# A two-layer hybrid block on one core: other start addresses for SBUF tiles, weight rows and inner tiles

## The chip, the core and the metric

The kernel runs on one core of a Trainium2 chip. Its five engines run side by side: TensorE (PE in the profile; its weight loads are listed as PEld) multiplies, VectorE (DVE) and ScalarE (ACT) work element by element, GpSimd (POOL) does some side work, and SyncE (SP) issues the loads and stores. The metric is the device time of one execution in microseconds (us).

A tile in SBUF is a run of bytes at the same offset in each of 128 partitions. This change is about these offsets. "A start of 32" below means an offset that is 32 bytes past a multiple of 128.

## What is computed

Two layers of a block on 512 tokens of 1024 features. Each layer adds two normed sublayers to x: a mixer (dilated attention beside a two-way mLSTM) and a gated feed-forward with a short convolution.

```python
def reference(x, ...):
    for l in range(DEPTH):
        mixed = hybrid_mixer(rms_norm(x, mix_pre_g[l]), w_in[l], ...)
        x = x + rms_norm(mixed, mix_post_g[l])
        ff = conv_ffn(rms_norm(x, ffn_pre_g[l]), w_up[l], ...)
        x = x + rms_norm(ff, ffn_post_g[l])
    return x

def hybrid_mixer(hn, w_in, ...):
    aq, ak, av, mq, mk, mv, mo, gates = jnp.split(hn @ w_in, split_at, axis=-1)
    ...
    return jnp.concatenate([attn, mlstm], axis=-1) @ w_out

def conv_ffn(hn, w_up, conv_w, conv_b, w_down):
    u = depthwise_conv_centred(hn @ w_up, conv_w, conv_b)
    gate, val = jnp.split(u, 2, axis=-1)
    return (jax.nn.gelu(gate, approximate=True) * val) @ w_down
```

The mixer's projections have 3600 columns, the feed-forward is 2816 wide, and everything is float32.

## The kernel before

Activations lie with the feature on partitions and the 512 tokens along the row, eight tiles of 128 features each. To keep float32 accuracy with the faster float32r products, each operand is split into a high and a low part, and `mac` (L193 to L202) makes three matmuls for each product: high weights with high activations, low weights with high activations, high weights with low activations. Of a matmul's two operands the *weights* are loaded into the array ahead of it (128 columns), and the *moving* operand streams through (up to 512 columns).

**Weights.** `load_raw` (L129) brings a piece of 128 by 1024 numbers (512 KB) into one of three buffers `wraw`, on SP's queue, in the order of use. `split_w` (L138) casts it to `whi` on ScalarE (L153) and subtracts on VectorE (`lo_part`, L91) to get `wlo`; both come from rings of three buffers of 4096 bytes a partition, eight rows of 128 numbers. Row k of a piece is the weight operand of the k-th of eight products that add up into one output tile.

```python
hi = whi_p.tile([P, 8, P], F32R, tag="whi", name="whi")
lo = wlo_p.tile([P, 8, P], F32R, tag="wlo", name="wlo")
```

**Activations.** The normed operand of a sublayer's first products is in eight pairs `ah`, `al` (2048 bytes each, `act_parts`); the mixer's output projection reads pairs `cp`. In the feed-forward, `unit` (L1038) makes 22 pairs `hh`, `hl` out of the gate and the value, and these are the moving operand of the down projection. A few pieces of weights that are split ahead of time lie in other tiles: `wnx`, `wsp`, `wlh`/`wll`, `pth`/`ptl`.

**Stages of a layer.** The mixer's 28 projection tiles, with attention and mLSTM steps as side work between the products; the output projection (8 tiles); the up projection (44 tiles of 8 times 3 matmuls of 512 columns); the down projection (8 tiles of 22 times 3). Near a norm, tiles are made by halves of the tokens, so with 256 columns. The value projection (`proj_v`) turns roles round: `ah` and `al` are the weights, 128 tokens at a time, and two rows of `whi` or `wlo` together are the moving operand of 256 columns, one run of 1024 bytes. Its outputs are scaled on VectorE in `v_out` (L657, L658).

**Order.** The program is written out step by step; side work is put in behind so many products (`settle`, `Stream.pump`), and a scheduler then orders each engine's instructions by its estimates. In the up and down projections TensorE runs the products one behind the other.

**Places.** Tiles come from pools that place them one behind the other. The granule is 32 bytes, so tiles of small or odd size shift all that follow them. [...]

Of the kernel before, what the change touches and what calls it, by code (L numbers as in the profile page):

```python
# [25 lines left out]
RAW = 3  # L26
RING = 3
# [5 lines left out]
# per head: the order of its projections (mLSTM q and k, both values, attention q and k), and its attention's rate  # L33
# [3 lines left out]
# columns of the per-feature parameter array  # L37
# [8 lines left out]
# columns of the constant array  # L46
# [10 lines left out]

@with_exitstack
def tile_hybrid_block(ctx: ExitStack, tc: tile.TileContext, xt, w_in, w_g, w_out, w_up, w_down, par, cst, out):
    nc = tc.nc  # L60
    pool = lambda name, bufs=1, **kw: ctx.enter_context(tc.tile_pool(name=name, bufs=bufs, **kw))
# [76 lines left out]
    def split_w(alloc=None):  # L138
        """the next piece as exact high and low parts; alloc gives their place, n of the eight rows at a time."""
        if not raw_q:  # L140
            return None
        raw, nk = raw_q.popleft()
        parts = {}
        n = 8
        k = 0
        while k < nk:
            if alloc is None:
                hi = whi_p.tile([P, 8, P], F32R, tag="whi", name="whi")
                lo = wlo_p.tile([P, 8, P], F32R, tag="wlo", name="wlo")
            else:  # L150
                hi, lo, n = alloc()
            m = min(n, nk - k)
            nc.scalar.copy(out=hi[:, 0:m, :], in_=raw[:, k:k + m, :])  # L153
            lo_part(lo[:, 0:m, :], raw[:, k:k + m, :], hi[:, 0:m, :])
            for j in range(m):
                parts[k + j] = (hi[:, j, :], lo[:, j, :])
            parts["all"] = (hi, lo)
            k += m
        load_raw()
        return parts  # L160
# [18 lines left out]
    # work to be put into the program once the tensor engine has so many more rows of products before it  # L179
# [12 lines left out]
    def mac(ps, w, kk, rhs, first, last, cols=None):  # L192
        """ps += w[:, kk, :]^T rhs with both operands as exact high and low parts."""  # L193
        settle()
        clock[0] += 3 * (T if cols is None else cols.stop - cols.start)
        hi, lo = w[kk]
        rh, rl = rhs
        if cols is not None:
            rh, rl = rh[:, cols], rl[:, cols]
        nc.tensor.matmul(out=ps, lhsT=hi, rhs=rh, start=first, stop=False)  # L200
        nc.tensor.matmul(out=ps, lhsT=lo, rhs=rh, start=False, stop=False)  # L201
        clock[1] = nc.tensor.matmul(out=ps, lhsT=hi, rhs=rl, start=False, stop=last).ins  # L202

# [1 line left out]
    class Stream:  # L205
        """generators one after another, a step at a time behind the products that come before it."""
# [29 lines left out]
    def rsqrt(ms, n):  # L236
        """1/sqrt(ms) on [P, n], by a first guess from the exponent and Newton steps."""
        y = sm.tile([P, n], F32, tag=f"rs_y{n}", name="rs_y")
        a = sm.tile([P, n], F32, tag=f"rs_a{n}", name="rs_a")
        yi = y[:, :].bitcast(I32)  # L240
        nc.vector.tensor_scalar(yi, ms.bitcast(I32), -0.5, float(0x5F3759DF), op0=ALU.mult, op1=ALU.add)
        for _ in range(3):
            nc.vector.tensor_tensor(out=a, in0=y, in1=y, op=ALU.mult)
            nc.vector.scalar_tensor_tensor(out=a, in0=a, scalar=-0.5, in1=ms, op0=ALU.mult, op1=ALU.mult)
            nc.vector.scalar_tensor_tensor(out=y, in0=a, scalar=1.5, in1=y, op0=ALU.add, op1=ALU.mult)
        return y

    def rsqrt_cols(ms):
        """for the two columns of ms [P, 2]: RS / sqrt(ms), by a first guess from the exponent and Newton steps."""
# [9 lines left out]
        # a third-order step, a = y^2 ms within 7% of 1: (a^2 + C1 a + C0) y = s / sqrt(ms)  # L259
# [4 lines left out]
        # Newton's: (y^2 ms - 3 s^2) y = -2 s^3 / sqrt(ms)  # L264
# [7 lines left out]
    class Stats:  # L272
        """Sums of squares over the features: the first tiles add up beside the tensor engine, which sums over the
        partitions of that sum and of each of the last `own` tiles."""
# [7 lines left out]
        def add(self, src, n, hf):  # L282
            """the n-th of the KT tiles, for the tokens of one half or (None) both."""
# [17 lines left out]
        def flush(self, h):  # L301
            """what has come for a half until now, the sum of the first tiles ahead."""
            if self.sp[h] is None:
                self.sp[h] = t_ps()
                nc.vector.memset(self.sp[h][:, 0:2], EPS)
                self.sums(h, 1, self.acc[:, halves[h]])
            for g, n, sq in self.late:
                if g == h:
                    self.sums(h, n - KT + self.own + 2, sq)
            self.late = [e for e in self.late if e[0] != h]  # L310
# [6 lines left out]
        def rstd(self, hf):  # L317
            """[P, 2] for a half, a token per partition."""
# [6 lines left out]
    def row_of(r):  # L325
        """[P, 2] with a token per partition -> [P, 256] PSUM with the token along the row, in every partition."""
# [11 lines left out]
    def pre_operand(g, k, ops, st, hf):  # L338
        """x * g as parts, and the square of x into the statistics."""
        parts_of(g, k, ops, hf)  # L340
        st.add(x[k][:, slice(0, T) if hf is None else halves[hf]], k, hf)
# [29 lines left out]
    class Post:  # L371
        """x += norm(m) * g for each half of the tokens, and the next block's operand from the new x."""
# [9 lines left out]
        def put(self, k, src, cols=slice(0, T)):  # L382
            """an output tile times the norm's gain."""
# [30 lines left out]
    def first_group(ws, pss, xp, scale, extra=None):  # L414
        """the tiles whose operand is still being made: by halves of the tokens, all tiles beside each other."""
# [10 lines left out]
    def last_tiles(ws, kts, act, post, n0, also=None):  # L426
        """the last output tiles by halves of the tokens, so that the norm of the first half overlaps the second."""
# [18 lines left out]
    def mixer_first(l, xp, sp, G, more, whole=False):  # L446
# [12 lines left out]
        if whole:  # L459
            # the input comes tile by tile  # L460
# [20 lines left out]
    def mixer(l, xp, first, mp, post):  # L481
# [10 lines left out]
        # what picks a direction's and head's own rows for the decay products: the chunk's m and, below, the chunk  # L492
# [18 lines left out]
        def gates(ps):  # L511
# [14 lines left out]
            # index: direction, step, head; the backward direction's step j is chunk 3 - j  # L526
# [6 lines left out]
            # log sigmoid(f) = min(f, 0) - log1p(exp(-|f|)), the log1p as 2 atanh(e / (2 + e))  # L533
# [32 lines left out]
            # running maxima, forward for the first 16 rows and backward for the others  # L566
# [19 lines left out]
            # the state's maximum before each step, and with the step's own  # L586
# [16 lines left out]
            # keys are twice their value until here, and carry the scale  # L603
# [3 lines left out]
            # rows: -M and m_prev - M in the chunk's own columns, as parts  # L607
# [22 lines left out]
        def conv_out(ps, i, name):  # L630
            """five taps, then twice the silu."""
# [15 lines left out]
        def v_out(pss):  # L647
            """values of both kinds with the token on partitions: [P, chunk, kind, feature], two chunks in a bank."""
# [22 lines left out]
        def rot_out(ps, name):  # L671
# [12 lines left out]
            if name == "aq":  # L684
                # a head's high and low parts on top of each other
# [3 lines left out]
            else:  # L689
                # a head's high part twice, and the low parts of both heads  # L690
# [11 lines left out]
        def attn(hp):  # L702
# [3 lines left out]
            def scores(a, qt):  # L706
# [7 lines left out]
                # -(s + bias) / 8 and its minimum  # L714
# [46 lines left out]
        def mlstm(h):  # L761
# [3 lines left out]
            # keys with the token on partitions, times what enters the state  # L765
# [32 lines left out]
            # the part that each direction sees  # L798
# [8 lines left out]
            for d in range(2):  # L807
# [7 lines left out]
                # the masked half may overflow, and is nothing in sm_  # L815
# [43 lines left out]
        # projections; side work of the heads goes between them  # L859
# [3 lines left out]
        # streams of side work, each with its steps for each part of a projection tile  # L863
# [15 lines left out]
        def proj_v():  # L879
            """the tokens as the output's rows: both kinds of values beside each other."""  # L880
# [3 lines left out]
            for c in range(4):  # L884
# [3 lines left out]
                for k in range(KT):  # L888
                    hi, lo = (w[:, 2 * (k % 4):2 * (k % 4) + 2, :].rearrange("p i f -> p (i f)") for w in ws[k // 4])
# [40 lines left out]
        # output projection  # L930
# [91 lines left out]
    def ffn(l, xp, first, fp, post):  # L1022
# [16 lines left out]
        def unit(i, pg, pv):  # L1039
# [4 lines left out]
            hi = fp.tile([P, T], F32R, name=f"hh{i}")  # L1044
            lo = fp.tile([P, T], F32R, name=f"hl{i}")
# [53 lines left out]
        def next_place():  # L1099
            k = places.pop(0)  # L1100
            return (fp.tile([P, 4, P], F32R, tag=f"hh{k}", name="wnx"), fp.tile([P, 4, P], F32R, tag=f"hl{k}", name="wnx"), 4)
# [8 lines left out]
    # loads in the order in which the first products need them  # L1110
# [26 lines left out]
    for l in range(DEPTH):  # L1137
        with tc.tile_pool(name=f"mix{l}", bufs=1) as mp:
            post = Post(l, "mix_post", l, "ffn_pre", 2)
# [5 lines left out]
        with tc.tile_pool(name=f"ffn{l}", bufs=1) as fp:  # L1145
            post = Post(l, "ffn_post", l + 1, "mix_pre", 1)
# [6 lines left out]
def _constants():  # L1153
# [32 lines left out]
    # how many of the dilated patterns hold key - query, as a bias before the scale  # L1186
# [63 lines left out]
```

## Time and profile before

| | us |
|---|---|
| Two runs | 1391.45 and 1391.57, median 1391.51 |
| Profiled execution, span from the first to the last instruction | 1389.7 |
| Mixer and output projection, layer 0 (0 to 390): TensorE busy | 377.62 |
| Mixer and output projection, layer 1 (690 to 1080): TensorE busy | 381.87 |
| Median of the runs above the profiled span | 1.8 |

The profiled execution's time outside its span isn't listed apart; the two runs stand 1.75 and 1.87 us above the span. How to read the rows: a row of busy times gives each engine's busy time in a stretch and, in brackets, how many of its instructions touch it. A timeline row is a start, a duration, engine, line, operation, and output<-inputs. A matmul's duration includes its way through the array, during which the next ones run already; the tempo is the distance between starts. A row of groups gives a count, the busy time in us, the mean of one in ns, and the idle time ahead of it.

### The profile page before, as it was taken

What the parts mean: (1) busy time and instruction counts of PE and PEld (TensorE: products, weight loads), DVE (VectorE), ACT (ScalarE), POOL (GpSimd) and SP (SyncE); (2) the same over time, 40 slices, a digit from 0 to 9 for tenths busy, and PEclk for the clock granted to TensorE, in tenths of its full rate; (3) what the DMA queues carried; (4) which work ended last, traced back from release to release, by engine and by line L of the source; (5) the groups of instructions that cost most, each with busy time, mean ns of one, the idle gap of its engine ahead of it and who ended that gap; (6) DMA issues with size and microseconds to landing.
All of it is one profiled execution on the core that took longest, in us unless ns stands there. A gap on an engine that the chain in (4) does not pass through costs nothing. (4 is left out here: it accounts for less than half of the span.)

```text
span 1389.7 us, 18680 instructions
## 1 busy us (share of the span) xinstructions
PE 1359.0 (98%) x7152; PEld 1126.2 (81%) x7152; DVE 955.7 (69%) x1885; ACT 721.8 (52%) x1226; POOL 105.9 (8%) x110
## 2 busy tenths in 40 slices
PE   7999999999999999999999999999999999999997
PEld 6778878789888888888986888787898888888886
DVE  6989788747887777422498887778479777773233
ACT  5686686754544444323356766866546444442230
POOL 0000000024000000000120000000240000000102
PEclk9999999999999999999999999999999999999999
DMA  6212122140333333233311121122412333323221
GB/s 231 61 35 88 31 61 77 48 150 2 100 98 107 91 95 99 86 96 103 99 67 61 61 61 51 42 77 74 124 47 76 107 91 96 102 87 99 90 89 61
DMA packets 34089, 115.34 MB, mean 83 GB/s; under 512 B 3664, under 2 KB 6352, under 8 KB 34000
## 3 DMA queue, kind: packets, MB, share of 16 engines
q1 hardware_dynamic: 34000, 114.15, 27.0%
q8 instruction: 56, 0.92, 0.3%
q14 instruction: 33, 0.27, 0.1%
HBM read 112.04 MB, written 2.10 MB: 82 GB/s over the span
## 5 line engine op out<-in xcount | busy, mean ns | idle before, releaser
L91 DVE TENSOR_TENSOR wlo<-wraw,whi 128x1024 fp32r<-128x1024 f32 (+1 forms) x192 | 236.5, 1234 | 180.6 <-ACT whi L153 178.8
L200 PE MATMUL mm<-ah,whi 128*128 128x512 f32 (+1 forms) x880 | 342.0, 389 | 0.0
L201 PE MATMUL mm<-ah,wlo 128*128 128x512 f32 (+1 forms) x880 | 335.3, 381 | 0.0
L202 PE MATMUL mm<-al,whi 128*128 128x512 f32 (+1 forms) x880 | 334.1, 381 | 0.9 <-DVE al L348 0.8
L153 ACT CAST whi<-wraw 128x1024 fp32r<-128x1024 f32 (+1 forms) x192 | 197.6, 1034 | 168.6 <-PE mm L202 112.4
L200 PEld LDWEIGHTS mm<-ah,whi 128*128 128x128 f32 x880 | 166.5, 189 | 39.1 <-issue 12.0
L202 PEld LDWEIGHTS mm<-al,whi 128*128 128x128 f32 x880 | 166.2, 189 | 32.3 <-issue 1.9
L201 PEld LDWEIGHTS mm<-ah,wlo 128*128 128x128 f32 x880 | 166.6, 189 | 27.8 <-issue 1.9
L296 POOL TENSOR_TENSOR acc<-acc,sq 128x512 f32<-128x512 f32 x22 | 29.6, 1345 | 764.1 <-ACT sq L293 759.8
L200 PE MATMUL mm<-hh,whi 128*128 128x512 f32 x220 | 86.7, 394 | 0.0
L201 PE MATMUL mm<-hh,wlo 128*128 128x512 f32 x220 | 86.7, 394 | 0.0
L202 PE MATMUL mm<-hl,whi 128*128 128x512 f32 x220 | 86.7, 394 | 0.0
L1029 DVE TENSOR_TENSOR u<-mm,prow 128x512 f32<-128x512 f32 x64 | 43.8, 686 | 50.1 <-PE mm L202 39.6
L893 PE MATMUL mm<-whi,ah 128*128 128x256 f32 x256 | 74.4, 292 | 0.2 <-DVE cu L633 0.2
L1046 ACT CAST hh<-cv 128x512 fp32r<-128x512 f32 x44 | 27.3, 620 | 87.5 <-DVE cv L1043 87.5
L895 PE MATMUL mm<-whi,al 128*128 128x256 f32 x256 | 72.4, 283 | 0.0
L894 PE MATMUL mm<-wlo,ah 128*128 128x256 f32 x256 | 72.4, 283 | 0.0
L1041 ACT ACTIVATE cg<-cg 128x512 f32<-128x512 f32 x44 | 27.9, 633 | 74.5 <-DVE cg L1035 74.2
L201 PE MATMUL o<-ah,wlo 128*128 128x512 f32 (+1 forms) x160 | 60.6, 379 | 0.0
L200 PE MATMUL o<-ah,whi 128*128 128x512 f32 (+1 forms) x160 | 60.5, 378 | 0.0
L202 PE MATMUL o<-al,whi 128*128 128x512 f32 (+1 forms) x160 | 60.5, 378 | 0.0
L719 ACT ACTIVATE p<-p,mx 128x512 f32<-128x512 f32 x64 | 46.1, 720 | 21.6 <-DVE mx L716 21.6
(317 smaller groups left out, 2788.3 us busy)
## 6 DMA issues: line engine op xcount, KB each, us to landing
wraw<-in_w_up SPq DMA_DIRECT2D x88, 512.0 KB, 3.6
wraw<-in_w_in SPq DMA_DIRECT2D x56, 512.0 KB, 3.5
wraw<-in_w_down SPq DMA_DIRECT2D x32, 512.0 KB, 3.5
wraw<-in_w_out SPq DMA_DIRECT2D x16, 512.0 KB, 3.5
wraw<-in_w_down SPq DMA_DIRECT2D x16, 384.0 KB, 3.1
x<-in_xt SPq DMA_DIRECT2D x4, 512.0 KB, 7.3
out_dram<-x SPq DMA_DIRECT2D x8, 256.0 KB, 2.2
tb<-in_cst SPq DMA_DIRECT2D x2, 967.0 KB, 5.1
```

Source lines behind the costliest of these rows:

```text
L91: nc.vector.tensor_tensor(out=dst, in0=src, in1=f32v(hi), op=ALU.subtract)
L153: nc.scalar.copy(out=hi[:, 0:m, :], in_=raw[:, k:k + m, :])
L200: nc.tensor.matmul(out=ps, lhsT=hi, rhs=rh, start=first, stop=False)
L201: nc.tensor.matmul(out=ps, lhsT=lo, rhs=rh, start=False, stop=False)
L202: clock[1] = nc.tensor.matmul(out=ps, lhsT=hi, rhs=rl, start=False, stop=last).ins
L296: e.tensor_tensor(out=self.acc[:, cols], in0=self.acc[:, cols], in1=sq, op=ALU.add)
L719: nc.scalar.activation(out=p_, in_=p_, func=AF.Exp, scale=-1.0, bias=mx, accum_out=den)
L893: nc.tensor.matmul(out=o_, lhsT=xh, rhs=hi, start=(k == 0), stop=False)
L894: nc.tensor.matmul(out=o_, lhsT=xh, rhs=lo, start=False, stop=False)
L895: clock[1] = nc.tensor.matmul(out=o_, lhsT=xl, rhs=hi, start=False, stop=(k == KT - 1)).ins
L1029: nc.vector.tensor_tensor(out=u, in0=ps, in1=st["row"], op=ALU.mult)
L1041: nc.scalar.activation(out=g, in_=g, func=AF.Gelu_apprx_tanh)
```

## The change

Five things change; the comments that the diff also drops do nothing.

- Every pool is wrapped in `Aligned`, which rounds each tile's size up to a multiple of 128 bytes. As the first tile starts at 0 of 128, so do the rest.
- The rows of `whi` and `wlo` are 136 numbers apart and not 128 (544 bytes, buffers of 4352); 128 of them are used. The cast, the subtraction and the moving operand of the value projection so become patterns of eight (or two) runs.
- `hh` and `hl` come from the unwrapped pool with 520 numbers a row, so each starts 32 bytes further than the one before it, modulo 128. The same holds for the two pairs `wnx` that take their place at the end.
- The value projection takes its two rows as a two-dimensional pattern.
- The scratch area shrinks from 16384 to 1024 bytes. 218752 bytes a partition are taken then.

```diff
+LINE = 128
+STEP = 8
...
+class Aligned:
+    def __init__(self, pool):
+        self.pool = pool
+    def tile(self, shape, dtype, **kw):
+        n = 1
+        for s in shape[1:]:
+            n *= s
+        if n * 4 % LINE == 0:
+            return self.pool.tile(shape, dtype, **kw)
+        flat = self.pool.tile([shape[0], -(-n * 4 // LINE) * LINE // 4], dtype, **kw)[:, 0:n]
...
-    pool = lambda name, bufs=1, **kw: ctx.enter_context(tc.tile_pool(name=name, bufs=bufs, **kw))
+    pool = lambda name, bufs=1, **kw: Aligned(ctx.enter_context(tc.tile_pool(name=name, bufs=bufs, **kw)))
...
-                hi = whi_p.tile([P, 8, P], F32R, tag="whi", name="whi")
-                lo = wlo_p.tile([P, 8, P], F32R, tag="wlo", name="wlo")
+                hi = whi_p.tile([P, 8, P + STEP], F32R, tag="whi", name="whi")[:, :, 0:P]
+                lo = wlo_p.tile([P, 8, P + STEP], F32R, tag="wlo", name="wlo")[:, :, 0:P]
...
-                    hi, lo = (w[:, 2 * (k % 4):2 * (k % 4) + 2, :].rearrange("p i f -> p (i f)") for w in ws[k // 4])
+                    hi, lo = (w[:, 2 * (k % 4):2 * (k % 4) + 2, :] for w in ws[k // 4])
...
-            hi = fp.tile([P, T], F32R, name=f"hh{i}")
-            lo = fp.tile([P, T], F32R, name=f"hl{i}")
+            hi = fp.pool.tile([P, T + STEP], F32R, name=f"hh{i}")[:, 0:T]
+            lo = fp.pool.tile([P, T + STEP], F32R, name=f"hl{i}")[:, 0:T]
...
+            mp = Aligned(mp)
...
+            fp = Aligned(fp)
...
-    nc = bacc.Bacc("TRN2", target_bir_lowering=False, num_devices=1)
+    nc = bacc.Bacc("TRN2", target_bir_lowering=False, num_devices=1, dynamic_dma_scratch_size=1024)
```

Starts modulo 128 as the two programs place them:

| Tile | before | after |
|---|---|---|
| ah, al, wlh, wll, prow, wraw, x | 32 | 0 |
| whi, wlo: rows 0 to 7 | all 32 | 0, 32, 64, 96, 0, 32, 64, 96 |
| hh, of i even / odd | 96 | 0 / 64 |
| hl, of i even / odd | 96 | 32 / 96 |
| cp (in turn on mixer tiles) | 32, 64 or 96 | 0 |
| pth, ptl, and attention's aq, ak | 64 | 0 |
| vs | 0 | 0 |
| wnx where it stands in tb's place | 96 | 0 |

The order of TensorE's, ScalarE's, GpSimd's and SyncE's instructions stays as it is. On VectorE three instructions move back in each layer. The place is the value projection of one head, where VectorE scales the product `mm` by `rt` into the mLSTM's values `v` and the attention's values `vf`, between steps of the mLSTM's output (`r`, `hs`) and of a softmax (`p`, `mx`, `den`). Before:

```order
L840 TENSOR_TENSOR r_1712<-s,ex 128x2
L650 MEMSET v_1777 128x4
L657 TENSOR_TENSOR v_1777<-mm,rt 128x2x128
L841 SCALAR_TENSOR_TENSOR r_1712<-s,r_1712 128x2
L658 TENSOR_TENSOR vf<-mm,rt 128x256
L842 RECIPROCAL r_1712<-r_1712 128x2
L716 ISA p,mx<-s,tb 128x512
L716 ISA mx 128x1
L844 SCALAR_TENSOR_TENSOR hs<-s,r_1712,hs 128x128
L657 TENSOR_TENSOR v_1777<-mm,rt 128x2x128
L658 TENSOR_TENSOR vf<-mm,rt 128x256
L720 RECIPROCAL den<-den 128x1
```

After, with lines 21 higher:

```order
L861 TENSOR_TENSOR r_1712<-s,ex 128x2
L671 MEMSET v_1777 128x4
L862 SCALAR_TENSOR_TENSOR r_1712<-s,r_1712 128x2
L678 TENSOR_TENSOR v_1777<-mm,rt 128x2x128
L863 RECIPROCAL r_1712<-r_1712 128x2
L737 ISA p,mx<-s,tb 128x512
L737 ISA mx 128x1
L865 SCALAR_TENSOR_TENSOR hs<-s,r_1712,hs 128x128
L679 TENSOR_TENSOR vf<-mm,rt 128x256
L678 TENSOR_TENSOR v_1777<-mm,rt 128x2x128
L741 RECIPROCAL den<-den 128x1
L679 TENSOR_TENSOR vf<-mm,rt 128x256
```

The scaling of the first two chunks into `v` stands one step later, that into `vf` behind the softmax step and `hs`, and the last one behind `den`. Elsewhere on VectorE only forms change, as here at the end of a mixer, where weights are split (`wlo`) behind steps of the attention. Before:

```order
L823 SCALAR_TENSOR_TENSOR Q_2789<-Q_2789,mq 128x512
L720 RECIPROCAL den<-den 128x1
L666 TENSOR_TENSOR sg<-mm,prow 128x512
L91 TENSOR_TENSOR ptl<-t,pth 128x4x128
L91 TENSOR_TENSOR wlo<-wraw,whi 128x1024
```

After:

```order
L844 SCALAR_TENSOR_TENSOR Q_2789<-Q_2789,mq 128x512
L741 RECIPROCAL den<-den 128x1
L687 TENSOR_TENSOR sg<-mm,prow 128x512
L112 TENSOR_TENSOR ptl<-t,pth 128x4x128
L112 TENSOR_TENSOR wlo<-wraw,whi 128x8x128
```

Nothing moved; the subtraction is written in eight runs of 128 numbers and not in one of 1024.

More of the change, by code (lines that the diff above doesn't have):

```diff
@@ L55 @@
 NC1 = CC["rowmask"]
+class Aligned:
[8 more added lines that the diff above has]
+        flat = self.pool.tile([shape[0], -(-n * 4 // LINE) * LINE // 4], dtype, **kw)[:, 0:n]
+        if len(shape) == 2:
+            return flat
+        names = " ".join("abcd"[:len(shape) - 1])
+        return flat.rearrange(f"p ({names}) -> p {names}", **{c: s for c, s in zip("abcd", shape[1:-1])})
 @with_exitstack
@@ L1100, in next_place @@
             k = places.pop(0)
-            return (fp.tile([P, 4, P], F32R, tag=f"hh{k}", name="wnx"), fp.tile([P, 4, P], F32R, tag=f"hl{k}", name="wnx"), 4)
+            return (fp.pool.tile([P, T + STEP], F32R, tag=f"hh{k}", name="wnx")[:, 0:T].rearrange("p (k m) -> p k m", k=4), fp.pool.tile([P, T + STEP], F32R, tag=f"hl{k}", name="wnx")[:, 0:T].rearrange("p (k m) -> p k m", k=4), 4)
         def also():
```

## The prediction

> **What bounds the kernel.** I read the page's busy times first, then its chain of waits, then the stages in the windows view, and at last single starts in the timeline of TensorE.
>
> ```profile
> span 1389.7 us, 18680 instructions
> PE 1359.0 (98%) x7152; PEld 1126.2 (81%) x7152; DVE 955.7 (69%) x1885; ACT 721.8 (52%) x1226; POOL 105.9 (8%) x110
> q1 hardware_dynamic: 34000, 114.15, 27.0%
> PE 36%; DVE 2%; ACT 0%; issue 0%; DVEq 0%
> ```
>
> TensorE is busy in 1359.0 of 1389.7 us, and no other engine comes near. The chain's shares are small because it could follow only part of the span, but nearly all of what it followed is TensorE. So time can come only from the tempo of the matmuls, and a busy share of 98% doesn't tell that tempo: matmuls overlap, so the number to read is the distance from one start to the next. The stages give it.
>
> ```profile
> core 0: us, PE busy (x) PEld busy (x) DVE busy (x) ACT busy (x) POOL busy (x), PEclk, DMA share, GB/s
> 390.00:560.00 170.00, 170.00 (x752) 140.77 (x751) 125.75 (x160) 76.55 (x95) 0.00 (x0) 1.00 0.33 98
> 570.00:670.00 100.00, 100.00 (x430) 80.17 (x429) 28.09 (x26) 29.05 (x39) 6.48 (x5) 1.00 0.35 107
> ```
>
> The first stretch is the up projection, the second the down projection of layer 0; both are pure streams of matmuls of 512 columns at a granted clock of 1.00. Two of the counted matmuls reach into a stretch from before it, so 170.00 / 750 = 226.7 ns from start to start, and 100.00 / 428.5 = 233.3 ns. The instruction, its shapes and the weights' tiles are the same. VectorE is far busier in the faster stretch (125.75 of 170 us against 28.09 of 100), so the other engines don't make the difference. What differs is where the moving operand starts: ah and al at 32 past a multiple of 128 bytes, hh and hl at 96. The timeline shows the step at the change of stage.
>
> ```profile
> 564.62 0.39 PE L201 MATMUL mm<-ah,wlo 128*128 128x512 f32 x1
> ...
> 565.75 0.39 PE L200 MATMUL o<-hh,whi 128*128 128x512 f32 x1
> ...
> 566.45 0.39 PE L200 MATMUL o<-hh,whi 128*128 128x512 f32 x1
> ```
>
> Five starts in 1.13 us (226), then three in 0.70 (233), with nothing between. So the start address matters. Matmuls of 256 columns say the same of the weights' address:
>
> ```profile
> 328.87 0.28 PE L200 MATMUL mm<-ah,wnx 128*128 128x256 f32 x1
> ...
> 329.21 0.28 PE L200 MATMUL mm<-ah,whi 128*128 128x256 f32 x1
> ...
> 330.17 0.28 PE L202 MATMUL o<-al,whi 128*128 128x256 f32 x1
> 673.91 0.28 PE L200 MATMUL mm<-hh,wlh 128*128 128x256 f32 x1
> ...
> 675.27 0.28 PE L200 MATMUL mm<-hh,wlh 128*128 128x256 f32 x1
> ...
> 678.11 0.28 PE L200 MATMUL mm<-hh,wlh 128*128 128x256 f32 x1
> ...
> 679.52 0.28 PE L200 MATMUL mm<-hh,wlh 128*128 128x256 f32 x1
> ```
>
> From wnx (weights at 96) three starts take 0.34 us, 113.3 ns each; from whi (weights at 32) eight take 0.96, 120.0 each. With hh moving, twelve take 1.36 (113.3); after a break the same twelve take 1.41 (117.5), so what came before counts too. Take ah with whi: 226.7 for 512 columns and 120.0 for 256 leave 106.7 for 256 columns, hence 213.3 for 512 and a fixed 13.3 on each matmul. The pairs 233.3/226.7 and 120.0/113.3 differ by the same 6.67, so I count in steps of 6.67 ns: two with ah and whi, three with hh at 512 columns, one with hh and with wnx at 256. None of these has zero.
>
> **The change part by part.** By the kernel's allocation ah, al, cp and nearly all other tiles will start at 0 of 128; the eight rows of whi and wlo at 0, 32, 64, 96 and again; hh at 0 or 64, hl at 32 or 96. No row before shows a moving operand of 256 or more columns at 0, so the price has to be bounded. The counts:
>
> ```profile
> L200 PE MATMUL mm<-ah,whi 128*128 128x512 f32 x768 | 309.5, 403 | 0.0
> L200 PE MATMUL o<-ah,whi 128*128 128x512 f32 x144 | 56.0, 389 | 0.0
> L200 PE MATMUL mm<-hh,whi 128*128 128x512 f32 x220 | 86.7, 394 | 0.0
> L200 PE MATMUL o<-hh,whi 128*128 128x512 f32 x88 | 34.7, 394 | 0.0
> L200 PE MATMUL mm<-cp,whi 128*128 128x512 f32 x80 | 31.5, 398 | 0.0
> L200 PE MATMUL mm<-ah,whi 128*128 128x256 f32 x112 | 32.5, 292 | 0.0
> L893 PE MATMUL mm<-whi,ah 128*128 128x256 f32 x256 | 74.4, 292 | 0.2 <-DVE cu L633 0.2
> ```
>
> Each stands for three (L201 and L202, or L894 and L895, have the same counts): 2736 matmuls of 512 columns from ah, 924 from hh, 240 from cp, 336 of 256 columns from ah, and 768 of 256 columns in the value projection, where the weights move.
>
> - Aligned ah, al, cp. Lower end: all steps go, 13.3 ns x 2976 = 39.7 us. Upper end: a third step as with hh, 6.67 x 2976 = 19.8 us more. I take one step off, which is a guess between the two: a start at a boundary should save one partial read, while whatever the weight load adds stays. 2976 x 6.67 = 19.8 us.
> - hh and hl spread over four starts: lower end 20.0 x 924 = 18.5 us off, upper end one step more, 6.2 us. I take one step off (to the 226.7 that ah has at another start): 6.2 us.
> - 336 short matmuls from ah: 120.0 to 113.3 as wnx shows, 2.2 us; upper end nothing.
> - Value projection: the moving operand becomes two runs of 512 bytes, the second at another start. Lower end 6.67 off as above, upper end one step more, 5.1 us either way. I take zero, since it gains an aligned ah as weights and loses a single run.
> - Rows of the weights apart: the cast and the subtraction write eight runs instead of one. Nearest rows:
>
> ```profile
> L91 DVE TENSOR_TENSOR wlo<-wraw,whi 128x1024 fp32r<-128x1024 f32 x178 | 218.3, 1229 | 136.8 <-ACT whi L153 134.9
> L91 DVE TENSOR_TENSOR ptl<-t,pth 128x512 fp32r<-128x512 f32 x64 | 43.7, 683 | 9.4 <-ACT pth L730 9.1
> L91 DVE TENSOR_TENSOR hl<-cv,hh 128x512 fp32r<-128x512 f32 x44 | 30.4, 690 | 22.0 <-ACT hh L1046 22.0
> L658 DVE TENSOR_TENSOR vf<-mm,rt 128x256 f32<-128x256 f32 x16 | 6.7, 416 | 0.0
> ```
>
> ptl is written in four runs and takes 683, hl in one and takes 690; their tiles start at 64 and 96. So neither runs nor starts cost VectorE anything, and I cost this at nothing; the cover is VectorE's 26% of free time in the up projection, where a subtraction would have to grow from 1.2 us by some 1.4 us to be late (44 us free over 31 pieces of weights). The three VectorE instructions that move back in each layer's value projection are of this 416 ns size, stand between others of their kind, and cost nothing. TensorE's order is unchanged. [...]
>
> Sum: 19.8 + 6.2 + 2.2 = 28.2 us off. Against the profiled span, 1389.7 - 28.2 = 1361.5; the runs' median of 1391.5 stands 1.8 us above the span, so 1363.3, rounded to 1363. If TensorE gains 3% in the up projection, VectorE's share rises from 74 to some 76% there, so nothing else is late next.
>
> [...]
>
> **The rivals.** *All steps go* (1331): 39.7 + 18.5 + 2.2 = 60.4 us off. For it: nothing in the program forces the 13.3. Against: no settled stream in the trace is without a step.
>
> *No net gain* (1393, from 1385 to 1410). The steps depend on how the two reads fall against each other, and staggered rows never let the stream settle. The trace shows such a state after a break:
>
> ```profile
> 57.99 0.39 PE L201 MATMUL mm<-ah,wlo 128*128 128x512 f32 x1
> ...
> 59.60 0.39 PE L202 MATMUL mm<-al,whi 128*128 128x512 f32 x1
> ...
> 61.87 0.39 PE L200 MATMUL mm<-ah,whi 128*128 128x512 f32 x1
> ```
>
> Seven starts take 1.61 us (230), the next ten 2.27 (227). At 230 everywhere the two up projections lose 3.3 x 1500 = 5.0 us and hh gains 3.3 x 924 = 3.0: 1393.5. With a third step for all of ah, 1410. Against it: this was a passing state, with equal starts.
>
> *Addresses do nothing*, 1391.5. It comes to the same class as the last. Against it stands the step at 565.75. [...]
>
> *Slower* (1430): a weight row that starts off 128 costs the stream two steps more. It strikes six rows in eight in all projections, 0.75 x 3900 matmuls x 13.3 = 39 us. It decides from 27.8 / 2925 = 9.5 ns each. For it: three steps occur. Against: weights at 32 are the present state, and at 96 they were faster.
>
> **How the numbers follow.** One step off 0.40, all steps 0.20, no net gain or no effect 0.30, slower 0.10. The 2% line, about what a measurement of this kernel can tell from no change, is 27.8 us, and the likeliest sum lies on it; since its open ends (hh, value projection) reach further down, I give 0.25 of its 0.40 to the faster side. Faster 0.25 + 0.20 = 0.45, within 2% 0.15 + 0.30 = 0.45, slower 0.10. The range leaves out the slow case and the worst of no net gain: 1330 to 1400. The likeliest case's own range is 1350 to 1375.
>
> **What would show it.** In the profile after: 220 ns from start to start in the up projection (about 773 matmuls in 170 us), 226.7 in the down projection, wlo still at some 1230 ns. Starts that swing about 230 speak for no net gain, 213 to 216 for all steps gone, 233 or more in the up projection for the slow case. The prediction is wrong if the tempo doesn't change, or if VectorE's or ScalarE's splits grow by over a microsecond.

## The result, and the profile after

| | before | after |
|---|---|---|
| Runs, us | 1391.45, 1391.57 | 1398.81, 1400.06 |
| Median, us | 1391.51 | 1399.43 |
| Span of the profiled execution, us | 1389.7 | 1396.8 |
| Ratio of the times, 95% interval | | 1.0057, 1.0038 to 1.0075 |

The changed kernel takes 7.9 us more. That is small, but the interval of the ratio lies wholly above 1: the kernel got slower, where 1363 us had been forecast. The page of the changed kernel, its span, busy times, data queue and the chain's shares by engine:

```profile
span 1396.8 us, 18682 instructions
...
PE 1365.5 (98%) x7152; PEld 1125.7 (81%) x7152; DVE 956.6 (68%) x1885; ACT 718.1 (51%) x1226; POOL 105.9 (8%) x110
...
q1 hardware_dynamic: 34000, 114.15, 27.0%
...
PE 36%; DVE 2%; ACT 0%; issue 0%; DVEq 0%
```

TensorE is the bound as before. Its busy time rose by 6.5 us, the span by 7.1, and no other engine changed by more than 4 us. The windows view of the same two stretches, the up and the down projection of layer 0:

```profile
core 0: us, PE busy (x) PEld busy (x) DVE busy (x) ACT busy (x) POOL busy (x), PEclk, DMA share, GB/s
390.00:560.00 170.00, 170.00 (x736) 137.99 (x736) 122.83 (x155) 74.56 (x94) 0.00 (x0) 1.00 0.32 94
570.00:670.00 100.00, 100.00 (x433) 80.97 (x432) 30.81 (x30) 29.05 (x39) 6.47 (x5) 1.00 0.35 105
```

The clock is 1.00 in both, as it was. By the prediction's way of counting, the up projection went from 752 matmuls (226.7 ns from start to start) to 736 (170.00 / 734 = 231.6), and the down projection from 430 (233.3) to 433 (100.00 / 431.5 = 231.7). The two stages, 6.7 ns apart before, now have nearly one tempo, between their old ones. The timeline of TensorE shows it in the up projection:

```profile
401.38 0.40 PE L221 MATMUL mm<-ah,whi 128*128 128x512 f32 x1
401.62 0.40 PE L222 MATMUL mm<-ah,wlo 128*128 128x512 f32 x1
401.85 0.39 PE L223 MATMUL mm<-al,whi 128*128 128x512 f32 x1
402.08 0.39 PE L221 MATMUL mm<-ah,whi 128*128 128x512 f32 x1
...
402.77 0.39 PE L221 MATMUL mm<-ah,whi 128*128 128x512 f32 x1
...
403.46 0.39 PE L221 MATMUL mm<-ah,whi 128*128 128x512 f32 x1
```

Three rows of weights (nine starts) from 401.38 to 403.46 take 2.08 us, 231 ns a start, and nothing is idle between them. The groups by form, of those the prediction priced:

```profile
L112 DVE TENSOR_TENSOR wlo<-wraw,whi 128x1024 fp32r<-128x1024 f32 x178 | 218.4, 1230 | 139.3 <-ACT whi L174 139.2
...
L112 DVE TENSOR_TENSOR ptl<-t,pth 128x512 fp32r<-128x512 f32 x64 | 43.7, 683 | 9.3 <-ACT pth L751 9.1
...
L914 PE MATMUL mm<-whi,ah 128*128 128x256 f32 x256 | 74.0, 290 | 0.2 <-DVE cu L654 0.2
```

The subtraction that makes wlo takes 1230 ns where it took 1229, now that it writes eight runs. So the loss is in TensorE's tempo. Summed up from the starts in the two traces, each matmul's distance to the next, in us:

| Matmuls | before | after | difference |
|---|---|---|---|
| up projection, 512 columns (1920) | 435.9 | 444.5 | +8.6 |
| down projection, 512 columns (924) | 215.6 | 214.5 | -1.1 |
| mixers without the output projection, all 512 columns (1088), waits included | 305.3 | 304.3 | -1.0 |
| value projection (768) | 95.6 | 94.7 | -0.9 |
| down projection, 256 columns (264) | 31.8 | 32.3 | +0.5 |

Together they give +6.1 of the 7.1. The rest is spread thinly over the span and was not followed further. The mixers' products with ah and al also got slower: their distances under 260 ns rose from 230.2 to 231.9 in the mean. But fewer starts were held up for longer than that (190 before, 183 after, 74.1 and 70.3 us together), so nothing of it stays.

### The profile page after: what moved, and what is told of

It reads as the page before. It is cut to its first block, busy times and chain, and to the rows that moved or that the text cites. A ratio compares the mean times of both kernels' runs of the same rounds, so it can differ in the third digit from the quotient of the medians.

```text
span 1396.8 us, 18682 instructions
## 1 busy us (share of the span) xinstructions
PE 1365.5 (98%) x7152; PEld 1125.7 (81%) x7152; DVE 956.6 (68%) x1885; ACT 718.1 (51%) x1226; POOL 105.9 (8%) x110
```

## The experiments

Three questions stood: which part of the change loses, what a start really does, and whether one can do better. The expectations give the theories by letters. S: a stream is fastest only where moving operand and weights all have one start, the same from row to row. Z: a start at 0 is costly by itself. E: each matmul pays by its own pair of starts. N: what counts is the pair of the moving operand and the *next* weights, which are loaded while it streams (in the trace of the kernel before the weights of the matmul that starts at 400.06 us are loaded from 399.84, while the one that starts at 399.83 runs for 0.39 us). C: only starts modulo 256 bytes matter, and that the rows are written and read in separate runs costs nothing.

**The change in parts.** Alignment alone, without the rows' and hh's extra 32 bytes; the rows alone; hh and hl alone.

```diff
 # aligned alone, against the changed kernel
-STEP = 8
+STEP = 0
 # rows alone, against the kernel before
-                hi = whi_p.tile([P, 8, P], F32R, tag="whi", name="whi")
+                hi = whi_p.tile([P, 8, P + 8], F32R, tag="whi", name="whi")[:, :, 0:P]
...
-                    hi, lo = (w[:, 2 * (k % 4):2 * (k % 4) + 2, :].rearrange("p i f -> p (i f)") for w in ws[k // 4])
+                    hi, lo = (w[:, 2 * (k % 4):2 * (k % 4) + 2, :] for w in ws[k // 4])
 # hh and hl alone, against the kernel before (hl and wnx likewise)
-            hi = fp.tile([P, T], F32R, name=f"hh{i}")
+            hi = fp.tile([P, T + 8], F32R, name=f"hh{i}")[:, 0:T]
```

Aligned alone:

> Every tile at a start of 0, but no spread: weight rows 512 bytes apart again, hh and hl at 0. Theory S (successive weight rows with different starts keep the stream from settling): the up projection settles again at 226.7 ns from start to start, because moving and weights have equal starts as they had before; hh and weights have equal starts too, so the down projection settles at 226.7 instead of 233.3 and the time is about 1391.5 - 924 x 6.67 ns = 1385 us. Theory Z (the start at 0 is itself the costly one): the up projection stays at about 231 ns and the time near 1399 us.

Rows alone:

> The kernel before with only the weight rows 32 bytes further apart (and the smaller scratch, which makes the room); all other tiles at their old starts. Theory S: the up projection at about 231 ns, the down projection between 230 and 233, the time 1391.5 + 1500 x 4.5 ns, and a little more in the mixers, so 1397 to 1400 us. Theory Z: nothing was aligned, so 226.7 and 233.3 ns and 1391.5 us.

hh and hl alone:

> The kernel before with only hh and hl 32 bytes further apart each (and the smaller scratch). Theory S: the up projection settled at 226.7 ns as before; the down projection doesn't settle, and swings about 230 to 233 ns; the time within 2 us of 1391.5. Theory Z: the same up projection, the down projection a mean of four starts, somewhere from 226.7 to 233.3, so 1385 to 1391.5 us.

| | median, us | ratio to before, 95% interval |
|---|---|---|
| aligned alone | 1387.12 | 0.9968 (0.9956 to 0.9981) |
| rows alone | 1398.65 | 1.0052 (1.0037 to 1.0067) |
| hh and hl alone | 1390.65 | 0.9994 (0.9985 to 1.0004) |

The windows of aligned alone (the second one ends at 660, so that only 512 columns lie in it):

```profile
390.00:560.00 170.00, 170.00 (x752) 140.84 (x751) 125.43 (x160) 77.11 (x96) 0.00 (x0) 1.00 0.33 97
570.00:660.00 90.00, 90.00 (x399) 74.56 (x398) 26.27 (x25) 27.04 (x36) 6.46 (x5) 1.00 0.33 99
```

Rows alone:

```profile
390.00:560.00 170.00, 170.00 (x736) 137.89 (x735) 122.81 (x156) 74.58 (x94) 0.00 (x0) 1.00 0.32 95
570.00:670.00 100.00, 100.00 (x433) 81.04 (x432) 30.72 (x30) 29.48 (x40) 6.46 (x5) 1.00 0.35 103
```

hh and hl alone:

```profile
390.00:560.00 170.00, 170.00 (x752) 140.79 (x751) 125.44 (x160) 76.78 (x95) 0.00 (x0) 1.00 0.32 98
570.00:670.00 100.00, 100.00 (x432) 81.06 (x432) 28.35 (x27) 29.39 (x39) 6.49 (x5) 1.00 0.36 108
```

The rows alone give the changed kernel's counts (736 and 433) and its whole loss. Alignment alone is faster than before: the up projection stays at 752, since ah and the weights had one start before (32) and have one now (0), and the down projection comes to 90.00 / 397 = 226.7 ns, since hh and hl now start where the weights do. That is 6.67 ns x 924 = 6.2 us; the span fell by 6.0, the medians of the runs by 4.4, less than S had forecast (1385 us). The 264 products of hh with 256 columns, whose starts are now equal too, got slower (31.8 to 32.7 us); what else keeps the medians closer was not followed. So a start at 0 neither costs nor saves anything (Z falls), and what counts is whether the starts are equal. hh and hl spread alone moves the down projection from 430 to 432, which the time can't show.

**A map of starts** (one run each). Weights' buffers at 0, 32 and 64 in turn, with hh and hl at 96; then weights' pieces at eleven offsets in turn against a moving operand at 0.

```diff
 # three starts, against aligned alone (wlo likewise; a filler of 96 bytes ahead of hh)
-                hi = whi_p.tile([P, 8, P + STEP], F32R, tag="whi", name="whi")[:, :, 0:P]
+                hi = whi_p.pool.tile([P, 8 * P + 8], F32R, tag="whi", name="whi")[:, 0:8 * P].rearrange("p (k m) -> p k m", k=8)
 # eleven offsets, in numbers of 4 bytes, against aligned alone; in layer 0 hi and lo, in layer 1 lo alone
+OFF = [0, 1, 2, 4, 8, 16, 24, 32, 40, 48, 56]
...
+                a, b = OFF[i % 11] if i < 104 else 0, OFF[i % 11]
+                hi = whi_p.tile([P, 8 * P + 64], F32R, tag="whi", name="whi")[:, a:a + 8 * P].rearrange("p (k m) -> p k m", k=8)
```

> A map of settled tempos: aligned tiles, weight rows 512 bytes apart, but the three ring buffers start at 0, 32 and 64 of 128, so that each piece of 24 matmuls has its own constant start; hh and hl all start at 96. Theory S: inside each piece the stream settles after a few matmuls to a value that belongs to the pair of starts; moving 0 with weights 0 gives 226.7 (equal starts), moving 96 with weights 32 gives 233.3 as before. If only the difference of the starts counts, moving 96 with weights 0 equals moving 32 with weights 64, which a second map can show. Theory Z: the up projection is at about 231 ns or more for every start of the weights.

> A finer map: all tiles aligned, weight rows 512 bytes apart, and each piece of weights is placed inside its buffer at 0, 4, 8, 16, 32, 64, 96, 128, 160, 192 or 224 bytes in turn; in layer 0 the high and the low part alike, in layer 1 the low part alone. Theory E (a matmul of 512 columns costs 226.7 ns where moving and weights have equal starts modulo 256 bytes, and 233.3 in the mean anywhere else): pieces at 0 at 226.7, all those from 32 to 224 at 233.3, 128 too; below 32 it is open. In layer 1 two of three matmuls keep equal starts, so about 229 if each matmul pays for itself. Theory S (a constant start settles at 226.7 whatever it is): 226.7 for every piece.

Times 1400.43 and 1400.19 us. The mean distance between starts inside undisturbed stretches of one kind, worked out from the traces, in ns, with the starts counted modulo 256:

| Moving at | weights at | ns |
|---|---|---|
| 0 | 0 | 226.7 |
| 0 | 32; 64 | 233.3; 233.4 |
| 96 | 0; 64 | 233.4; 233.3 |
| 96 | 32 | 230.8 (229 in some pieces, 233.3 in the others) |
| 0 | 4; 8; 16; 32 | 232.5; 230.7; 233.5; 233.4 |
| 0 | 64; 96; 128; 160 | 233.5; 234.3; 233.4; 233.3 |
| 0 | 192; 224 | 229.0; 233.3 |

Equal starts stand alone at 226.7. An offset of 4 bytes costs nearly as much as one of 128, so it is no matter of distance, and 128 bytes apart is as bad as 32, so the modulus is not 128; that 256 is enough, the control further down shows.

The values well below 233 are no leftovers of a stream that has yet to settle: their distances repeat. At 192 they go 226, 229, 232 ns again and again, at 8 they go 229, 229, 234, 230, 231, to within a nanosecond. So one unequal start does not cost what another does. The pair of 96 and 32 shows that the pair alone doesn't decide either: some of its pieces of weights run at 226, 229, 232, and others at 233, 233, 234, each throughout. The expectation had 233.3 for it, as before; but counted modulo 256 the kernel before has hh at 96 with weights at 160, another pair. What chooses between the two cycles is open. In layer 1, with only the low parts off, two of three matmuls in each row have equal starts; E gave about 229 there, and the stretches show some 230.5 to 233.5. One unequal matmul spoils its equal neighbours too.

**Half of the rows equal; all of them equal, but changing.** Rows 128 bytes further apart (starts 0 and 128 modulo 256, hh and hl unspread); then the changed kernel's rows with ah, al, hh and hl spread alike, so that the moving operand of row k starts where row k does; then with the moving operand where the next weights lie.

```diff
 # rows 128 apart, against the changed kernel (hh, hl and wnx with T)
-STEP = 8
+STEP = 32
 # matched, against the changed kernel: ah and al of row k both at 32 k; hh likewise
-        lo = base.tile([P, T], F32R, tag=f"xl{k}", name="al")
+        lo = base.pool.tile([P, T + STEP], F32R, tag=f"xl{k}", name="al")[:, 0:T]
...
-            hi = fp.pool.tile([P, T + STEP], F32R, name=f"hh{i}")[:, 0:T]
+            hi = fp.pool.tile([P, T], F32R, name=f"hh{i}")
 # next weights, against the changed kernel: ah at 32 k, al at 32 (k + 1); hh, hl likewise
-        hi = base.tile([P, T], F32R, tag=f"xh{k}", name="ah")
+        hi = base.pool.tile([P, T + STEP], F32R, tag=f"xh{k}", name="ah")[:, 0:T]
...
-            lo = fp.pool.tile([P, T + STEP], F32R, name=f"hl{i}")[:, 0:T]
+            lo = fp.pool.tile([P, T], F32R, name=f"hl{i}")
```

> All tiles aligned, hh and hl without spread, and the weight rows 128 bytes further apart in place of 32: their starts are then all 0 modulo 128, but in turn 0 and 128 modulo 256. Theory E with 256 bytes: every second row is unequal, so the up projection is at 230.0 ns, the down projection at 230.0, and the time about 1391.5 + 1500 x 3.3 ns - 924 x 3.3 ns = 1393 us or up to 2 more. The same theory with 128 bytes: 226.7 in both and 1385 to 1387 us, as with rows 512 bytes apart. Theory S with starts modulo 256: unsettled, 230 to 232 ns.

> The weight rows stay 32 bytes further apart as in the change, but al's and hl's tiles too are 32 bytes longer, so that the activations of row k (ah, al, or hh, hl) start at the same place modulo 256 as row k of the weights. Each matmul so has equal starts, but the start moves on by 32 bytes every three matmuls. Theory E (each matmul's own pair of starts decides): 226.7 ns in the up and the down projection, and about 1385 to 1388 us. Theory S (the stream must have constant starts from one matmul to the next, because the next weights are read while the present operand moves): not settled, or settled above 226.7: 228 to 232 ns and 1392 to 1400 us.

> As the matched spread, but with the 32 bytes added to ah and hh in place of al and hl, so that each moving operand starts at the same place modulo 256 as the weights of the NEXT matmul, which are read while it moves: high weights k+1 behind al of row k, low and high weights k behind ah of row k. A matmul's own pair is unequal in one of three cases. Theory N (what counts is the moving operand against the weights being loaded beside it): all but a few are equal, so the streams settle at 226.7 ns in the up projection and nearly so in the down projection, and the time is 1386 to 1389 us. Theory S (starts must be constant from row to row, whatever is equal): about 231 ns and 1397 to 1400 us, as with the matched spread.

| | median, us | ratio to before, 95% interval |
|---|---|---|
| rows 128 apart | 1400.10 | 1.0060 (1.0042 to 1.0078) |
| matched | 1398.55 | 1.0049 (1.0035 to 1.0063) |
| next weights | 1398.58 | 1.0049 (1.0032 to 1.0066) |

The up projection of each, first with rows 128 apart:

```profile
390.00:560.00 170.00, 170.00 (x736) 137.75 (x735) 122.51 (x156) 74.28 (x94) 0.00 (x0) 1.00 0.32 95
```

Matched:

```profile
390.00:560.00 170.00, 170.00 (x736) 137.85 (x735) 123.23 (x157) 73.43 (x93) 0.00 (x0) 1.00 0.32 96
```

Next weights:

```profile
390.00:560.00 170.00, 170.00 (x736) 138.12 (x736) 122.80 (x156) 74.56 (x94) 0.00 (x0) 1.00 0.31 95
```

Three layouts, one count. With rows 128 apart, half of the products have equal starts; paid pair by pair that is 230.0 ns, and it is 231.6. In the matched kernel every single matmul has equal starts, and by E all should run at 226.7. N falls in the same way. The timeline of the matched kernel, the first matmul of some of its rows:

```profile
402.30 0.39 PE L221 MATMUL mm<-ah,whi 128*128 128x512 f32 x1
402.53 0.40 PE L222 MATMUL mm<-ah,wlo 128*128 128x512 f32 x1
402.76 0.39 PE L223 MATMUL mm<-al,whi 128*128 128x512 f32 x1
402.99 0.39 PE L221 MATMUL mm<-ah,whi 128*128 128x512 f32 x1
...
403.69 0.39 PE L221 MATMUL mm<-ah,whi 128*128 128x512 f32 x1
...
404.38 0.39 PE L221 MATMUL mm<-ah,whi 128*128 128x512 f32 x1
...
405.07 0.39 PE L221 MATMUL mm<-ah,whi 128*128 128x512 f32 x1
```

Each row takes 0.69 us (2.77 for four) where three times 226.7 is 0.68. At the trace's full resolution the three distances are 228 to 229, 235 and 231 ns in turn: the change of start from one row to the next costs 14 ns a row, even where both operands change alike. Of the theories stated, S is what remains. In the mean over the up projection of layer 0, the changed kernel, the rows alone, the matched one and the next weights all take 694.2 ns a row. The weights' start moves on by 32 bytes a row in all four, while the moving operand's start stays in two of them and moves in the other two; it makes no difference to the sum. Why it doesn't is open.

**Is it the start, or the separate runs?** The control: the rows alone again, but 256 bytes further apart. The splits write eight runs as there, and every start modulo 256 is what it was in the kernel before.

```diff
 # against rows alone (whi and wlo)
-                hi = whi_p.tile([P, 8, P + 8], F32R, tag="whi", name="whi")[:, :, 0:P]
+                hi = whi_p.tile([P, 8, P + 64], F32R, tag="whi", name="whi")[:, :, 0:P]
```

> A control: the kernel before with the weight rows 256 bytes further apart (768 in place of 512) and the smaller scratch. The cast, the subtraction and the value projection's moving operand have the same patterns of separate runs as in the change, but every start modulo 256 stays what it was. Theory C (only starts modulo 256 matter to TensorE, and the separate runs cost nothing): 226.7 ns in the up and 233.3 in the down projection, and 1390 to 1393 us. If the separate runs or the distance of the rows cost something by themselves: the up projection above 226.7 ns or idle time on TensorE, and 1395 us or more.

1391.53 us, ratio 0.9998 (0.9988 to 1.0007). The two windows:

```profile
390.00:560.00 170.00, 170.00 (x752) 140.77 (x751) 126.15 (x161) 76.17 (x94) 0.00 (x0) 1.00 0.32 97
570.00:670.00 100.00, 100.00 (x430) 80.17 (x429) 28.77 (x27) 28.63 (x38) 6.48 (x5) 1.00 0.35 107
```

752 and 430, the counts of the kernel before. So C holds: separate runs cost nothing, and the whole loss of the change is that its rows' starts differ modulo 256.

**A better version.** All tiles at multiples of 256, rows together; then the same with the pieces of weights that only 256-column matmuls use moved off by 64 or 192 bytes, since those matmuls were faster with unequal starts already in the profile before (120.0 against 113.3 ns).

```diff
 # all at 256, against the changed kernel
-LINE = 128
-STEP = 8
+LINE = 256
+STEP = 0
 # and short ones apart (lo likewise): offsets in numbers of 4 bytes, by the piece's place in the order of use
+OFF = {**{j + l: 16 for l in (0, 104) for j in (2, 3, 10, 11, 14, 15, 22, 23)}, **{j: 48 for j in (36, 37, 38, 39, 104, 105, 140, 141, 142, 143)}}
...
+                hi = whi_p.tile([P, 8 * P + 64], F32R, tag="whi", name="whi")[:, a:a + 8 * P].rearrange("p (k m) -> p k m", k=8)
```

> All tiles at the same start modulo 256 bytes (they were so modulo 128 in the aligned kernel without spread, which left half of cp and some side tiles 128 off), weight rows 512 apart, no spread. Both theories: up and down projection at 226.7 ns, cp from 233.3 to 226.7 (1.6 us). If equal starts of the side work's tiles let the mixers' streams settle sooner as well, 1300 matmuls from about 231 to 227 give up to 5 us more: 1380 to 1386 us. If not, 1385 to 1387.

> As the kernel with all tiles at one start modulo 256, but the pieces of weights that serve only matmuls of 256 columns lie 64 bytes off (moving operand 64 bytes behind the weights' start, modulo 256): the value projections, the first four tiles of each up projection and the second mixer's first two. Before, the short matmuls took 120.0 ns with equal starts and 113.3 to 117.5 with 64 bytes between. Both theories: 2.5 to 6.7 ns less on some 1100 short matmuls, 3 to 7 us less than the kernel without that. If side work between them spoils it, the same time.

| | median, us | ratio to before, 95% interval |
|---|---|---|
| all at 256 | 1388.14 | 0.9974 (0.9963 to 0.9985) |
| all at 256, short ones apart | 1383.61 | 0.9944 (0.9931 to 0.9958) |

All at 256 brings the streams from cp, which aligned alone had left 128 bytes apart from the weights, from 231 to 228 ns; that is 1 us, less than these intervals can tell. Against aligned alone (1387.12) no gain shows, and 1388.14 lies above both of its forecasts (1380 to 1386, or 1385 to 1387). The groups by form show the value projection and the short products, first of all at 256:

```profile
L914 PE MATMUL mm<-whi,ah 128*128 128x256 f32 x256 | 74.4, 292 | 0.2 <-DVE cu L654 0.2
...
L221 PE MATMUL mm<-ah,whi 128*128 128x256 f32 x112 | 32.5, 292 | 0.0
```

With the short ones apart:

```profile
L919 PE MATMUL mm<-whi,ah 128*128 128x256 f32 x256 | 73.5, 288 | 0.2 <-DVE cu L659 0.2
...
L226 PE MATMUL mm<-ah,whi 128*128 128x256 f32 x112 | 31.6, 285 | 0.0
```

Summed up from the starts in the two traces, the value projection takes 93.3 us where it took 95.7, and the 384 short products of the up projections take 49.1 where they took 49.8. Together that is 3.1 us, and the spans of the two profiled executions are 3.1 us apart; the medians are 4.5 apart, and the rest is not in these traces. Counting only distances under 160 ns, so that no start that was held up is among them, the mean falls from 119.7 to 116.4 ns in the value projection and from 119.6 to 116.3 in the short products of ah with whi and wlo. The short products of hh kept equal starts (32.8 us, and 31.8 in the kernel before), so something was left. This version is the fastest of all, 8.0 us below the kernel before as it ran beside it (1391.63).

## Why the prediction was wrong, step by step

**What bounds the kernel** was right: TensorE's tempo in its streams, at a clock of 1.00, with the other engines beside it.

**"Aligned ah, al, cp" is the step that failed.** It took 6.67 ns off 2976 matmuls because "a start at a boundary should save one partial read", a guess; no run here shows such a read. Aligned alone shows 226.7 ns in the up projection, 0 off, not 6.67. The starts as such do nothing; equal ones do, and ah and the weights were equal before. The mistake began in the reading. Before, ah at 32 with weights at 32 ran at 226.7, and hh at 96 with weights at 32 at 233.3. The prediction read this as the moving operand's start ("So the start address matters") and counted steps from it; the difference of the two starts explains it as well, and none of the rows that the prediction shows parts the two. A place that it left out could have: behind the first products of the up projections, 48 matmuls of 512 columns take ah, at its usual start, with weights in wnx, which here start at 64.

```profile
350.53 0.40 PE L201 MATMUL t<-ah,wnx 128*128 128x512 f32 x1
...
353.09 0.39 PE L200 MATMUL s<-ah,whi 128*128 128x512 f32 x1
```

Eleven starts take 2.56 us, 233 ns each, though the moving operand is where it is in the stream of 226.7.

The count of steps leaned on the short matmuls as well: 226.7 less 120.0, both with equal starts, gave a "fixed 13.3". The same subtraction with the unequal starts of hh, 233.3 less 113.3, gives 120.0 for 256 columns and would leave a fixed part below nothing. Unequal starts make 512 columns slower (226.7 to 233.3) and 256 columns faster (120.0 to 113.3), so the two don't count in the same steps, and "none of these has zero" promised time that no layout tried here found. The count of 2976 also leaves out 144 matmuls from ah and cp that are written to other tiles; at 6.67 ns that is 1 us and changes nothing.

**The same step missed the rows.** The spread of the weights' rows was costed on VectorE and ScalarE, and in the likeliest case nothing was charged for it on TensorE. There it breaks the stream: 231.5 instead of 227.0 ns on 1920 matmuls of the up projection, 8.6 us.

That 1399.4 lies just inside the range of 1330 to 1400 is no merit of the sum: the range reached up there for a rival, not for the likeliest case, whose own range ended at 1375.

**hh and hl spread**: forecast 226.7 and 6.2 us off, measured 232 and 1.1. The 6.2 us are there (aligned alone has them), but only by giving hh and hl the weights' start with rows together.

**Short matmuls from ah**: 2.2 us off forecast, and next to nothing came. The 384 of the up projections take 49.5 us before and 49.3 after; with all starts equal (aligned alone) they take 49.7, so what little there is comes from the rows' unequal starts and not from the alignment. The 128 at the start of the second mixer, the gates' among them, take 20.2 us both times. Single distances mislead there: in the trace of the kernel before the granted clock is 0.50 from 700.3 to 703.7 us, and its starts in that stretch are 213 ns apart; the changed kernel's trace has no such stretch there, and its matmuls wait instead.

**Value projection**: nothing forecast, 0.9 us off. With all starts equal it stays at 95.6 us (aligned alone), so this too comes from the rows' unequal starts.

**The splits and the moved instructions** were rightly costed at nothing, and the scratch rightly has no term in the sum: wlo 1230 against 1229 ns, ptl 683 both times, the scaling into vf 417 against 416, and the rows 256 apart, with the smaller scratch, at 1391.53 us show the eight runs free on their own.

**The rivals.** *No net gain* came true, in its mechanism and its sign: "staggered rows never let the stream settle". It gave 230 ns, 5.0 us lost in the up projections and 3.0 gained by hh, 1393; measured were 231.5, 8.6 and 1.1, 1399.4. Its size was low since it counted 1500 matmuls where 1920 are concerned, and took its tempo from a passing state. At 0.30 it was held less likely than the guess of a saved read, because its row had equal starts; but that row did show a stream that hadn't settled, and the guess had no row at all. *All steps go* and *slower* had no part in it: no stream of 512 columns in any kernel here was faster than 226.7 ns, and the changed up projection went to 231.5. *Addresses do nothing* is excluded by rows alone against rows 256 apart, 1398.65 and 1391.53.

## What to carry to other kernels

Give the moving operand and the weights of a long stream of 512-column matmuls one start modulo 256 bytes, and keep it from row to row; here that is worth 6.7 ns of 233 on each. Matmuls of 256 columns gained here from unequal starts (119.7 to 116.4 ns in the value projection). A layout that spreads rows over several starts gave up the settled stream here even where each pair is equal (694 ns a row, and not 680). And when two stages differ in two things at once (the moving operand's start, and its difference from the weights'), make a run that parts them before building a sum on either.

## What the runs showed of the hardware

- A float32r stream of 512 columns has 226.7 ns from start to start with equal starts modulo 256 bytes, and 229 to 234 with constant unequal ones, from an offset of 4 bytes on; most have 233.
- With unequal starts the distances run in short cycles that repeat, and one and the same pair can run in either of two (226, 229, 232 or 233, 233, 234 ns).
- Successive rows are tied to each other: equal pairs whose start moves by 32 bytes a row take 694 ns for three matmuls, and not 680. What in the chip ties them was not shown.
- At 256 columns it is the other way round: unequal starts are faster, by some 3.3 ns in the version with the short ones apart (119.7 to 116.4 in the value projection).
- In the trace of the kernel before the granted clock fell to 0.50 for 3.4 us in the middle of the execution, at 700.3 us; starts of 256 columns were 213 ns apart then.
- A plain float32 product was slower than a float32r one: the four of 128 columns in L795 are eight matmuls in the trace of the kernel before, whose first seven distances from 47.78 us on take 0.78 us, 111 ns each, so some 222 ns a product, where a float32r product of 256 columns takes 120.0.
- VectorE's subtraction and ScalarE's cast didn't feel the starts or the runs: wlo takes 1230 ns in eight runs and 1229 in one, and the cast to whi 1047 in eight and 1050 in one, in these two rows, after and before.

```profile
L174 ACT CAST whi<-wraw 128x1024 fp32r<-128x1024 f32 x178 | 185.5, 1047 | 175.6 <-PE mm L223 118.2 <-PE o L223 43.6 <-PE mm L916 10.7
```

```profile
L153 ACT CAST whi<-wraw 128x1024 fp32r<-128x1024 f32 x178 | 185.9, 1050 | 166.7 <-PE mm L202 110.5 <-PE o L202 41.5 <-PE mm L895 11.5
```
